# Two layers of mixer and expert stage on one core: modulation columns read two visits after their DMAs, and more ticks between the parts of the second mixer's coroutines

## The chip, the core and the metric

The kernel runs on one core of a Trainium2 chip. The metric is device time in microseconds for one launch, the median of several runs. The core has TensorE (PE for its matmuls, PEld for its weight loads), VectorE (DVE), ScalarE (ACT), GpSimd (POOL) and SyncE (SP), which here only issues DMAs. Each engine works through its own queue in order and waits on semaphores for the others.

## The reference, cut to what matters

Two layers over 512 tokens of width 1024, in fp32. The first layer's mixer is `mixer_ab` (a gated linear recurrence beside chunked gated linear attention), the second's is `mixer_c` (a gated delta rule with 8 heads of 128). Each layer ends in 32 experts in 4 groups, two experts per token.

```python
cond = silu(c)
for layer in range(2):
    mod = cond @ w_ada[layer] + b_ada[layer]          # 6 vectors of 1024 per layer
    sh1, sc1, gt1, sh2, sc2, gt2 = split(mod, 6)
    u = rms_norm(h, norm1[layer]) * (1 + sc1) + sh1
    m = mixer_ab(u, ...) if layer == 0 else mixer_c(u, ...)
    h = h + gt1 * m
    u = rms_norm(h, norm2[layer]) * (1 + sc2) + sh2
    h = h + gt2 * hier_moe(u, ...)                    # 32 experts, top 2 of one group
return rms_norm(h, final_norm)
```

In `mixer_c` each head solves a triangular system in every chunk, and then runs a recurrence over the chunks:

```python
v_new = u_c - w_c @ state
o     = (q * exp(g)) @ state + (q @ k.T * decay) @ v_new
state = state * exp(g_last) + (k * exp(g_last - g)).T @ v_new
o     = head_rms_norm(o, norm_g) * silu(z)            # then @ w_out
```

## The kernel before

**Steps and ticks.** A mixer is a list of steps, run in order by `run_steps` (line 491). A step splits a block of weights into a high and a low part (`split`, lines 423 and 424: ACT copies the high part, POOL subtracts to get the low one) and then issues matmuls of 128x512, three for each product (lines 430 to 432). After every six of these matmuls the step yields, which is one tick of the stream (`Stream`, line 49). All other work of a mixer is in Python generators, here called coroutines, which the stream resumes: a generator that yields n is resumed n ticks later. So a number behind a `yield` says how many groups of six matmuls are written into the program between one part of a coroutine and the next. Once the steps of a list are used up, `flush` and `until` go on ticking with no matmuls in between, until the generators that must be finished are finished.

**Order.** That fixes the order in which the program is written. A planner then puts each engine's instructions in order with its own costs, by the written order as priority among those that it holds to be ready, so small shifts against the written order occur. On the chip each engine's queue runs strictly in that order: an instruction whose input is late holds up everything behind it on its engine.

**Modulation vectors.** `mods` (line 317) works on the vectors (layer, index) that are not needed at once: six in the first mixer, four in the second. One vector takes four visits, in each of which eight small matmuls (line 258) multiply the condition into one 1 MB tile of `w_ada`. After the second and the fourth visit ACT copies 512 results into `modrow` (line 348) and issues two or four small DMAs (line 355) which gather them into rows of a stack tile `modst`, one buffer for each of two shapes. `finish` transposes the stack on PE (line 296 or 303) and lets DVE add it up into columns (lines 308 and 310). A vector is finished in the visit right after its fourth one (`made[0][0] < n`); visits are three or four ticks apart in the first mixer (`M0`), six in the second (`M1`). The last vector has no next visit: it is finished four ticks after its last one. Before the output projection `build` waits until the stream's queue is empty.

**Second mixer.** Its 20 units are k, q, z, v for four groups of two heads, and four quarters of the output projection; each unit of the first kind is 48 step matmuls per pair of tiles and heads, 8 ticks. The coroutines per head are `keys`, `queries` and `values`; `logits` computes the gates once and sets `gates_known`, for which `keys` waits. When a group's two heads have their keys, `solve` starts: it waits `g.wait` ticks (22, 22, 18, 22), then until the group before it has been solved, and then goes through five parts up to `recurrence`. For each of the four chunks after the first, `recurrence` has three parts: the state product (line 1186, with DVE's `rr_` at 1188), the solve (1195, with DVE's `vn` at 1197), and the outputs (1203, 1212, 1214); after the outputs it spawns `head_out`, which normalises on ACT and DVE (894 to 907), yields `HO`, transposes (911) and splits the result for the output projection (915 to 917). `head_out` serves the first mixer's attention as well. The last quarter of the output projection (`fin`, 48 step matmuls) is run by `build` after all coroutines of the mixer have ended, and brings in the router and the experts' pools.

**Experts.** `moe` runs 16 pairs of experts, lines 1455 to 1608; its weights come as 1 MB DMAs on SP's queue into 17 or so buffers as they come free.

Of the kernel before, what the change touches and what calls it, by code (L numbers as in the profile page):

```python
# [33 lines left out]
W0 = 8, 6  # L34
W1 = 10

LL, LK, K2, LV, LQ, HO, A1, A2, GL = 3, 5, 3, 6, 4, 3, 3, 2, 3
M0, M1 = (3, 4, 4), (6,)
WAIT = 22, 22, 18, 22

# [10 lines left out]
class Stream:  # L51
# [2 lines left out]


    def __init__(self):
        self.n, self.c, self.q, self.front = 0, 0, [], 0

    def spawn(self, gen, lag=0, back=False):
        self.front += not back  # L60
        self.push(gen, lag, back)
        self.run()

    def push(self, gen, lag, back):
        self.c += 1
        heapq.heappush(self.q, (self.n + lag, self.c, gen, back))

    def run(self):
        while self.q and self.q[0][0] <= self.n:
            _, _, gen, back = heapq.heappop(self.q)  # L70
            lag = next(gen, None)
            if lag is None:
                self.front -= not back
            else:
                self.push(gen, lag, back)

    def tick(self):
        self.n += 1
# [11 lines left out]
class Build:  # L90
# [224 lines left out]
    def mods(self, vs, pool, ahead, pace, then={}):  # L315


        seq = [(l, v, hb, i) for l, v in vs for hb in range(2) for i in range(2)]
        tiles = []

        def issue():
            if len(tiles) < len(seq):
                l, v, hb, i = seq[len(tiles)]
                src = self.a["w_ada"][l][512 * i:512 * i + 512, v * D + hb * 512:v * D + hb * 512 + 512]
                tiles.append(self.load(src, 512, pool))

        def finish():
            _, l, v, st = made.pop(0)
            self.mod_finish(l, v, st)
            if (l, v) in then:  # L330
                after.append(then[l, v])
        for _ in range(ahead):
            issue()
        made, after = [], []
        for n, (l, v, hb, i) in enumerate(seq):
            yield pace[n % len(pace)]
            if not i:
                p = self.ps()
            self.mod_rows(p, tiles[n], 4 * i, not i, i == 1)
            tiles[n] = None  # L340
            issue()
            while after:
                after.pop()()
            if made and made[0][0] < n:
                finish()
            if i:
                rows = self.mix.tile([P, 512], F32, name="modrow", tag="modrow")
                self.nc.scalar.activation(rows, p, AF.Copy)
                if not hb:
                    st = self.mod_stack(v)  # L350

                m, w = st.shape
                for j in range(m // 8):
                    r = m // 2 * hb + 4 * j
                    self.nc.scalar.dma_start(st[r:r + 4], rows[::32, w * j:w * j + w])
                if hb:
                    made.append((n, l, v, st))
        for _ in range(len(made)):
            yield 4
            finish()  # L360
        while after:
            yield 3
            after.pop()()

    def mod_stack(self, v):

# [553 lines left out]
    def mixer_c(self, u, es, right, second):  # L920
# [45 lines left out]
        def logits():  # L966

            p = self.narrow(u, wba)
            bap = ep.tile([P, T], F32, name="bap", tag="kn", bufs=1)
            nc.vector.tensor_copy(bap, p)  # L970
            yield 2
            p = self.ps([P, NT, 16])
            for t in range(NT):
                nc.tensor.matmul(p[:, t], bap[:, t * P:(t + 1) * P], self.fold[:, :16], start=True, stop=True)
            with tc.high_priority(PRI):
                nc.vector.tensor_add(xa_, p[:, :, 8:16], prm[:, None, 8:16].to_broadcast([P, NT, 8]))
                nc.vector.scalar_tensor_tensor(gd, xa_, -1.0, xa_, op0=OP.mult, op1=OP.max)
                nc.scalar.activation(gd, gd, AF.Exp, scale=-1.0)
                nc.scalar.activation(prm[:, 0:8], prm[:, 0:8], AF.Exp)
                nc.scalar.activation(beta, p[:, :, 0:8], AF.Exp, scale=-1.0)  # L980
                nc.scalar.activation(gd, gd, AF.Ln, bias=self.one)
            nc.vector.tensor_scalar(beta, beta, 1.0, None, op0=OP.add)
            nc.vector.reciprocal(beta, beta)
            nc.vector.scalar_tensor_tensor(gd, xa_, 0.0, gd, op0=OP.max, op1=OP.add)
            nc.vector.scalar_tensor_tensor(gd, gd, -1.0, prm[:, None, 0:8].to_broadcast([P, NT, 8]),
                                           op0=OP.mult, op1=OP.mult)
            yield LL
            with tc.high_priority(PRI):
                nc.vector.tensor_copy(gd40[:, :, 32:40], gd)
                p = self.ps([P, NT, 40])  # L990
                pl = self.ps([P, NT, 8])
                nc.tensor.matmul(p, tri, gd40, start=True, stop=True)
                nc.tensor.matmul(pl, self.ones, gd, start=True, stop=True)
                nc.vector.tensor_copy(gc40, p)
                pr = self.ps([40, T])
                for t in range(NT):
                    nc.tensor.matmul(pr[:, t * P:(t + 1) * P], gc40[:, t], self.ident, start=True, stop=True)
                nc.scalar.activation(grow, pr, AF.Copy)
                nc.vector.tensor_sub(grow[32:40], pr[32:40], grow[32:40].bitcast(F32))
            nc.vector.tensor_copy(egl, pl)  # L1000
            nc.vector.tensor_copy(egn, p[:, :, 0:8])
            nc.vector.tensor_sub(ehat, egl, gc)
            nc.scalar.activation(ex, ex, AF.Exp)
            nc.vector.tensor_scalar(egn, egn, -1.0, None, op0=OP.mult)
            self.gates_known = True
            first_columns()

# [62 lines left out]
        def queries(h, hd, p, g):  # L1070
            qT = conv_silu(p, h, "qT", ep)
            sq = ep.tile([P, T], F32, name="sq", tag="vT", bufs=1)
            nc.gpsimd.tensor_mul(sq, qT, qT)
            sums = self.column_sums(sq, ep)
            next(sums)
            yield LQ
            while not hd.keyed:
                yield 1
            nc.gpsimd.tensor_mul(hd.qg, hd.qg, qT)
            p = self.ps([P, NT, P])  # L1080
            for t in range(NT):
                nc.tensor.matmul(p[:, t], hd.kT[:, ts(t)], qT[:, ts(t)], start=True, stop=True)
            nc.vector.tensor_mul(hd.E, p, hd.E)
            p = next(sums)

            if g.eq is None:
                g.eq = hp.tile([P, NT, HG], F32, name="eq", bufs=3)
            nc.vector.tensor_scalar(g.eq[:, :, h % HG], p, P * EPS, P * EPS * EPS, op0=OP.mult, op1=OP.add)
# [11 lines left out]
        def solve(g):  # L1100
# [27 lines left out]
            for b in range(4):  # L1128
                src = Yt[sb[b]].rearrange("p c u -> p u c")
                nc.vector.transpose(XT[sb[b], :, sb[b]], src)  # L1130
                nc.scalar.activation(X[sb[b], :, sb[b]], src, AF.Copy)
            yield 1

            lo32 = slice(0, 32)
            pP = self.ps([P, U, 32])
# [37 lines left out]
        def recurrence(g):  # L1173
# [5 lines left out]
            for t in range(NT):  # L1179
# [8 lines left out]
                    nc.vector.scalar_tensor_tensor(r, p, hd.sc[:, 2, t:t + 1], hd.vb[:, t], op0=OP.mult, op1=OP.add)  # L1188
                    R.append(r)
                if t:  # L1190
                    yield 1
                VN = []
                for hh in range(HG):
                    p = self.ps([P, P])
# [616 lines left out]
    def build(self):  # L1811
# [4 lines left out]
        with ExitStack() as es0:  # L1816
# [8 lines left out]
            for l in range(2):  # L1825
                with ExitStack() as es:
                    self.mix = self.pool(es, "mix%d" % l, 2, **right_side)
                    self.whl = self.pool(es, "whl%d" % l, 3, **right_side)
                    right = self.pool(es, "right%d" % l, 1, **right_side)
                    self.stream = st = Stream()  # L1830
                    with ExitStack() as ms:
                        ut = [self.uroom.tile([P, 4, T], F32R, name="w", tag="w") for _ in range(4)]
                        u = lambda i, k, ut=ut: ut[2 * i + k // 4][:, k % 4]
                        vp = self.pool(ms, "v%d" % l, 2 - l)
                        us = ExitStack()
                        tmp = self.pool(us, "ut%d" % l, 1, **right_side)
                        if l == 0:
                            fin = self.mixer_ab(u, ms, right, *self.startup(u, tmp, us, vp))
                        else:
                            fin = self.mixer_c(u, ms, right, self.restart(u, tmp, us, vp))  # L1840
                        st.until(lambda: not st.q)
                    os_ = ExitStack()
                    self.moe_open(l, os_)
                    self.run_steps(st, fin)
                    st.until(lambda: not st.q)
                self.dump_h("hm%d" % l)
                self.moe(os_)
                if l:
                    self.finish()
                os_.close()  # L1850
                self.dump_h("ho%d" % l)
# [137 lines left out]
```

## Time and profile before

| what | value |
| --- | --- |
| median of 3 runs | 1714.82 us (1712.03 to 1715.41) |
| profiled execution | 1716.33 us, of which 1714.6 us are the span of the instructions |
| mean granted clock of TensorE | 0.978 of full speed |
| first mixer | from 0 to about 300 us |
| first expert stage | from about 320 to 800 us |
| second mixer | from about 815 to 1200 us |
| second expert stage | from about 1210 to 1700 us |
| DMA in the expert stages | 411 to 413 GB/s |

A row of the waits names the instruction that waited, what it waited for, and the time in total, how often, and the longest. A row of the timeline has the start, the duration, engine, line, operation, output<-input and shape; in brackets is the idle time of the engine before it. A matmul's duration includes its way through the array: matmuls start every 0.23 us while each is shown with 0.39 us.

### The profile page before, as it was taken

Reading aid. Unit: us, or ns where it says so; the run is one execution under the profiler, and the core shown is the slowest. Engines: PE = TensorE matmul, PEld = TensorE weight load, DVE = VectorE, ACT = ScalarE, POOL = GpSimd, SP = SyncE. Lnnn points to the kernel's source line nnn. Section 1 sums busy time; section 2 is a strip of 40 time slices with the busy share of each in tenths; the row PEclk is TensorE's granted clock in tenths of the full one; section 3 lists DMA queues with packets and bytes.
Section 4 is the critical chain, followed back from the end, with each engine's and each line's share of the span. In section 5 each row is a group of like instructions: output and inputs, shape, how many; then the busy total and the mean of one; then the engine's idle time right before and its main releaser. Section 6 shows DMA issues by size and latency. Waiting matters only on the chain. (4 is left out here: it accounts for less than half of the span.)

```text
span 1714.6 us, 23030 instructions
## 1 busy us (share of the span) xinstructions
PE 1630.9 (95%) x8890; PEld 979.8 (57%) x8890; DVE 766.4 (45%) x1770; ACT 522.6 (30%) x1033; POOL 396.1 (23%) x346
## 2 busy tenths in 40 slices
PE   6999998899999999998999999999899999999996
PEld 3665666544554555454666766778454555455453
DVE  3345543432433224244687787755424334243324
ACT  4665322310110111013746566554210111011013
POOL 2464442210010101001544343443110101001011
PEclk9999998999999999999899999999999999999998
DMA  8765645699999999995244433156689999999992
GB/s 304 228 222 170 248 149 196 233 361 379 412 413 411 414 411 413 413 411 172 75 138 134 149 99 122 52 187 246 255 355 409 413 411 413 412 412 413 412 406 99
DMA packets 156561, 496.02 MB, mean 289 GB/s; under 512 B 16472, under 2 KB 43668, under 8 KB 141088
## 3 DMA queue, kind: packets, MB, share of 16 engines
q1 hardware_dynamic: 155488, 493.23, 74.9%
q8 instruction: 72, 1.18, 0.3%
q10 hardware_dynamic: 960, 1.28, 0.2%
q14 instruction: 41, 0.34, 0.1%
HBM read 492.21 MB, written 2.10 MB: 288 GB/s over the span
## 5 line engine op out<-in xcount | busy, mean ns | idle before, releaser
L1531 PE MATMUL ps<-w,XTm 128*64 128x512 f32 x2048 | 447.2, 593 | 0.0
L1531 PEld LDWEIGHTS ps<-w,XTm 128*64 128x64 f32 x2048 | 161.7, 137 | 267.6 <-issue 260.5
L424 POOL TENSOR_TENSOR wlo<-w,whi 128x512 fp32r<-128x512 f32 x136 | 181.5, 1340 | 249.2 <-ACT whi L423 231.3
L1585 PE MATMUL ps<-w,hT 128*64 128x512 f32 (+1 forms) x1056 | 229.2, 583 | 1.0 <-ACT hT L1563 1.0
L1554 DVE TENSOR_TENSOR gg<-gg,ps 128x512 f32<-128x512 f32 x32 | 22.0, 689 | 377.4 <-PE ps L1531 377.3
L430 PE MATMUL ps<-w,whi 128*128 128x512 f32 x384 | 162.9, 425 | 0.7 <-ACT w L552 0.7
L431 PE MATMUL ps<-w,whi 128*128 128x512 f32 x384 | 154.6, 403 | 2.2 <-POOL w L554 1.5
L1585 PEld LDWEIGHTS ps<-w,hT 128*64 128x64 f32 x1056 | 81.8, 136 | 128.9 <-issue 116.0
L432 PE MATMUL ps<-w,wlo 128*128 128x512 f32 x384 | 154.1, 402 | 0.0
L1608 DVE TENSOR_TENSOR w<-w,ps 128x512 f32<-128x512 f32 (+1 forms) x248 | 149.4, 664 | 6.9 <-PE ps L1599 5.5
L1540 POOL CAST sel<-ident 32x128 fp32r<-32x128 f32 x32 | 9.0, 282 | 591.9 <-PE ps L1568 533.8
L1589 POOL TENSOR_TENSOR yl<-y,yh 128x512 fp32r<-128x512 f32 x60 | 76.6, 1276 | 249.6 <-ACT yh L1588 249.6
L1588 ACT ACTIVATE yh<-y 128x512 fp32r<-128x512 f32 (+1 forms) x66 | 40.8, 618 | 293.7 <-DVE y L1587 292.7
L423 ACT ACTIVATE whi<-w 128x512 fp32r<-128x512 f32 x136 | 84.6, 627 | 146.1 <-PE ps L431 76.0
L1455 PE MATMUL ps<-Dm,hhi 128*128 128x256 f32 x512 | 126.7, 289 | 0.0
L1455 PE MATMUL ps<-Dm,hlo 128*128 128x256 f32 x512 | 123.9, 284 | 0.0
L1587 DVE SCALAR_TENSOR_TENSOR y<-ps,wsl,gate 128x512 f32<-128x512 f32 (+1 forms) x66 | 48.5, 735 | 149.8 <-issue 76.2
L1455 PEld LDWEIGHTS ps<-Dm,hhi 128*128 128x128 f32 x512 | 101.9, 200 | 13.5 <-issue 13.5
L1599 PE MATMUL ps<-yh,dt 128*128 128x512 f32 (+1 forms) x264 | 105.9, 406 | 0.0
L1563 ACT ACTIVATE hT<-ps 128x512 f32<-128x512 f32 x32 | 19.1, 598 | 284.2 <-PE ps L1561 265.9
L1455 PEld LDWEIGHTS ps<-Dm,hlo 128*128 128x128 f32 x512 | 101.8, 199 | 0.2
L1599 PE MATMUL ps<-yl,dt 128*128 128x512 f32 (+1 forms) x264 | 100.9, 387 | 0.0
(522 smaller groups left out, 2356.4 us busy)
## 6 DMA issues: line engine op xcount, KB each, us to landing
w<-in_moe_w_dram SPq DMA_DIRECT2D x380, 1024.0 KB
w<-in_w_ada_dram SPq DMA_DIRECT2D x40, 1024.0 KB
w<-in_w_in_c_dram SPq DMA_DIRECT2D x16, 1024.0 KB
w<-in_w_in_ab_dram SPq DMA_DIRECT2D x10, 1024.0 KB
wst<-in_w_ada_dram SPq DMA_DIRECT2D x8, 1024.0 KB
w<-in_w_out_ab_dram SPq DMA_DIRECT2D x4, 1024.0 KB
w<-in_moe_w_dram SPq DMA_DIRECT2D x8, 512.0 KB
w<-in_w_out_c_dram SPq DMA_DIRECT2D x4, 1024.0 KB
```

Of the source, the lines that this page charges most:

```text
L423: nc.scalar.activation(hi, src, AF.Copy)
L424: nc.gpsimd.tensor_sub(lo, src, hi.bitcast(F32))
L430: mm(p, lhs[0], rhs[0], start=start, stop=False)
L431: mm(p, lhs[0], rhs[1], start=False, stop=False)
L432: mm(p, lhs[1], rhs[0], start=False, stop=stop)
L1455: nc.tensor.matmul(p, spread(src[:, t], k // 4)[k % 4], Dm[:, t].rearrange("p e s -> p (e s)"), start=t + i == 0, stop=t == NT - 1 and i == 1)
L1531: self.nc.tensor.matmul(ps[j][half[e]], X[:, k, half[e]], w, start=k == 0, stop=k == KD - 1)
L1585: nc.tensor.matmul(py[half[e]], hT[:, k, half[e]], w, start=k == 0, stop=k == 3)
L1587: nc.vector.scalar_tensor_tensor(y32, py, wsl, gate[:, c], op0=OP.mult, op1=OP.mult)
L1589: (nc.vector if last else nc.gpsimd).tensor_sub(yl[:, c], y32, yh[:, c].bitcast(F32))
L1599: mm = nc.tensor.matmul(p, dt[:, t * P:(t + 1) * P], y[:, s], start=i == 0, stop=i == 1)
L1608: nc.vector.tensor_add(h, h, p)
```

## The change

`mods` finishes a vector one visit later (`n - 1`), and hands the last vector to a generator `rest`, pushed with a lag of 8 ticks and marked `late`: `build` no longer waits for it before the output projection. The constant `HO` goes from 3 to 4. `logits` yields two ticks before it sets `gates_known`; `queries` yields two ticks between its product with the keys and the matmuls of its column sums; `solve` yields two ticks instead of one behind the copies into `X` and `XT`; `recurrence` yields two ticks instead of one between the state product and the solve, in the second to the fourth chunk. No instruction is added or removed.

```diff
-LL, LK, K2, LV, LQ, HO, A1, A2, GL = 3, 5, 3, 6, 4, 3, 3, 2, 3
+LL, LK, K2, LV, LQ, HO, A1, A2, GL = 3, 5, 3, 6, 4, 4, 3, 2, 3
...
-        self.n, self.c, self.q, self.front = 0, 0, [], 0
+        self.n, self.c, self.q, self.front, self.late = 0, 0, [], 0, 0
...
-    def push(self, gen, lag, back):
+    def push(self, gen, lag, back, late=False):
         self.c += 1
-        heapq.heappush(self.q, (self.n + lag, self.c, gen, back))
+        self.late += late
+        heapq.heappush(self.q, (self.n + lag, self.c, gen, back, late))
...
-            if made and made[0][0] < n:
+            if made and made[0][0] < n - 1:
                 finish()
...
-        for _ in range(len(made)):
-            yield 4
-            finish()
-        while after:
-            yield 3
-            after.pop()()
+
+        def rest():
+            while made or after:
+                while after:
+                    after.pop()()
+                if made:
+                    finish()
+                yield 6
+        self.stream.push(rest(), 8, True, True)
...
             nc.vector.tensor_scalar(egn, egn, -1.0, None, op0=OP.mult)
+            yield 2
             self.gates_known = True
...
             nc.vector.tensor_mul(hd.E, p, hd.E)
+            yield 2
             p = next(sums)
...
                 nc.scalar.activation(X[sb[b], :, sb[b]], src, AF.Copy)
-            yield 1
+            yield 2
...
                 if t:
-                    yield 1
+                    yield 2
                 VN = []
...
-                        st.until(lambda: not st.q)
+                        st.until(lambda: len(st.q) == st.late)
                     os_ = ExitStack()
```

## Rows read from the trace of the kernel before

**Rows 1.** The page's busy times by engine, with their share of the span.

```profile
PE 1630.9 (95%) x8890; PEld 979.8 (57%) x8890; DVE 766.4 (45%) x1770; ACT 522.6 (30%) x1033; POOL 396.1 (23%) x346
```

**Rows 2.** The page's costliest groups: the experts' matmuls; last figure: idle before.

```profile
L1531 PE MATMUL ps<-w,XTm 128*64 128x512 f32 x2048 | 447.2, 593 | 0.0
```

**Rows 3.** Waits of PE in the first mixer, 45 to 300 us.

```profile
PE ps L303 <- DMA modst<-modrow: 4.8, 1, 4.8
PE ps L296 <- DMA w<-in_w_ada_dram: 2.9, 1, 2.9
```

**Rows 4.** Waits of PE in the second mixer, 760 to 1200 us.

```profile
PE ps L284 <- DVE xr L280: 3.9, 6, 1.2
PE ps L911 <- ACT orow L907: 2.4, 2, 1.9
PE ps L1139 <- ACT X L1131: 2.3, 2, 2.0
PE ps L1038 <- DVE grow L999: 2.0, 1, 2.0
PE ps L1195 <- DVE rr__7207 L1188: 1.6, 1, 1.6
...
PE ps L303 <- DMA modst<-modrow: 0.8, 1, 0.8
...
PE ps L1195 <- DVE rr__8078 L1188: 0.5, 1, 0.5
```

**Rows 5.** Stretches: length, busy time by engine, granted clock (sixth), DMA share, GB/s.

```profile
148.60:151.50 2.90, 0.02 (x1) 0.00 (x0) 2.90 (x5) 1.11 (x4) 2.02 (x1) 0.99 0.73 283
151.50:154.90 3.40, 3.36 (x9) 2.78 (x10) 3.40 (x8) 2.96 (x6) 1.92 (x2) 0.50 0.01 2
...
264.10:274.30 10.20, 5.40 (x15) 4.04 (x15) 1.94 (x9) 0.63 (x1) 1.26 (x1) 0.50 1.00 413
...
847.80:854.60 6.80, 6.80 (x18) 4.88 (x17) 4.90 (x15) 6.73 (x16) 4.56 (x5) 0.50 0.33 116
...
1021.90:1028.70 6.80, 6.04 (x19) 4.87 (x19) 5.15 (x23) 0.78 (x3) 0.01 (x1) 0.50 0.03 8
...
1127.70:1131.10 3.40, 3.40 (x12) 2.71 (x11) 0.83 (x3) 1.76 (x8) 1.56 (x2) 0.50 0.00 0
```

**Rows 6.** Timeline of all engines at the end of the first mixer.

```profile
258.34 0.16 DVE L409 SCALAR_TENSOR_TENSOR or<-rsz,or 128x4 f32<-128x4 f32 x1
...
258.86 1.30 POOL L424 TENSOR_TENSOR wlo<-w,whi 128x512 fp32r<-128x512 f32 x1 [2.30 <-ACT whi L423]
...
258.93 1.24 DVE L409 SCALAR_TENSOR_TENSOR or<-rsz,or 128x4 f32<-128x4 f32 x1
...
262.52 2.37 ACTq L355 DMA_DIRECT2D modst<-modrow  x4
...
263.82 1.25 PE L911 MATMUL ps<-ident,orow 128*128 128x128 f32 x4 [2.00 <-DVE orow L905]
...
267.06 1.26 POOL L917 TENSOR_TENSOR yBlo<-yf,yBhi 128x512 fp32r<-128x512 f32 x1 [4.17 <-ACT yBhi L916]
```

**Rows 7.** PE by line, 1175.55 to 1194.6 us; one of three like rows.

```profile
L430 PE MATMUL ps<-whi,ychi 128*128 128x512 f32 x18 | 7.3, 405 | 0.0
```

**Rows 8.** Timelines at the end of the second mixer: PE, ACT, POOL.

```profile
1170.80 0.39 PE L1214 MATMUL ps<-Sc,qg 128*128 128x128 f32 x2
...
1175.16 0.38 PE L911 MATMUL ps<-ident,orow 128*128 128x128 f32 x2
...
1172.65 0.62 ACT L907 ACTIVATE orow<-ps,or 128x128 f32<-128x128 f32 x2 [0.23 <-DVE or L901]
...
1177.10 0.73 POOL L917 TENSOR_TENSOR yclo<-yf,ychi 128x256 fp32r<-128x256 f32 x1 [1.05 <-ACT ychi L916]
```

**Rows 9.** Timelines of DVE and ACT around the fourth z tile of the second mixer.

```profile
959.98 0.34 DVE L915 SCALAR_TENSOR_TENSOR yf<-ps,cv,Z 128x128 f32<-128x128 f32 x1
...
960.79 0.60 ACT L1233 ACTIVATE Z<-ps 128x512 f32<-128x512 f32 x1
```

More of the change, by code (lines that the diff above doesn't have):

```diff
@@ L62, in spawn @@
         self.run()
-    def push(self, gen, lag, back):
+    def push(self, gen, lag, back, late=False):
         self.c += 1
-        heapq.heappush(self.q, (self.n + lag, self.c, gen, back))
+        self.late += late
+        heapq.heappush(self.q, (self.n + lag, self.c, gen, back, late))
     def run(self):
         while self.q and self.q[0][0] <= self.n:
-            _, _, gen, back = heapq.heappop(self.q)
+            _, _, gen, back, late = heapq.heappop(self.q)
+            self.late -= late
             lag = next(gen, None)
@@ L74, in run @@
             else:
-                self.push(gen, lag, back)
+                self.push(gen, lag, back, late)
     def tick(self):
```

## The prediction

> **What bounds the kernel now.** I read the page's busy times first: PE is busy in 1630.9 of 1714.6 us, twice as long as the next engine, DVE [rows 1]. PE's matmuls in the experts have no idle time before them [rows 2], so that stage lasts as long as its matmuls, and whatever a mixer saves reaches the end of the kernel. The 84 us in which PE is idle are the place to look; the waits of PE, asked for each mixer alone, say what ends them. In the first mixer two waits stand out, both ahead of transposes of a modulation stack, 4.8 and 2.9 us [rows 3]. The second is put down to a load of `w_ada`, but the instruction reads only `modst` and a constant, so I read it as a wait for the small DMAs into `modst`. In the second mixer the waits are spread over the places that the change touches: column sums 3.9 us, the `head_out` transposes 2.4, the solve's first products 2.3, the gates' rows 2.0, the chunks' solves four times from 1.6 to 0.5, together 3.7, and one modulation stack 0.8 [rows 4]. That is 15.1 us.
>
> A wait costs more than itself. The stretches show the granted clock falling to 0.50, the lower of its two levels (1.2 GHz), for a while behind such a gap: right behind the 2.9 us one, behind the one of 4.8, and at four places of the second mixer [rows 5]. Work done at half clock takes twice its time, so half of PE's busy time in such a stretch is lost: 1.7 us of 3.36 in the first; in the second mixer half of 6.80, 6.04 and twice 3.40 (the row of one of these two stands), together 9.8 us.
>
> **The change part by part.** No instruction is added. Each yield puts six more step matmuls, 6 x 0.23 = 1.4 us at full clock, between an instruction and the one that reads it.
>
> *A vector finished one visit later, first mixer.* The transposes at 151.5 us [rows 3, 5] move behind the next visit, three or four ticks and so 4 us or more later, when their data has landed. Gone: 2.9 us of wait and 1.7 us of clock, 4.6. Below: 0, if the late data was that of another queue and the next instruction waits for it; above: 4.6. I take 4.6, since the DMAs are what the transpose reads. The stack has one buffer per shape, so for three of the ten vectors the next vector's small DMAs now wait for the transpose of the same visit, and behind them ACT's next `split` copy; the transpose follows that visit's matmuls while ACT still copies `modrow`, so nothing (bounds 0 and 3 x 0.3). The router's preparation, which runs behind the vector of shifts, comes one visit later, at 14 of 24, still far ahead of the router. On SP's queue nothing changes its order, since the loads are asked for in the visit before `finish` in either version.
>
> *The first mixer's last vector.* Its four DMAs leave ACT from 262.52 to 264.89 us; PE ends its `head_out` transposes at 265.07 [rows 6] and then stands for 4.8 us in front of the stack [rows 3], with the output projection's last quarter queued behind. With `rest` the transpose comes 8 ticks later, inside that quarter, and costs there the 0.28 us that it costs now. The projection can start at 265.07 instead of 270.1. What is late next is `yBlo` of the last chunk, ready at 268.32 [rows 6]; but nine matmuls for the other three chunks come first, which take some 3.4 us at half clock (nine in the 3.40 us from 151.5 on [rows 5]), and only the third matmul behind them reads it. So 5.0 us are gained. Of the half-clock stretch [rows 5] the matmuls from 270.09 on lie in it for 4.2 us, so 2.1 are lost now; the gap of 2.0 us ahead of the transposes [rows 6] stays, and elsewhere a gap of this size is followed by at least 3.4 us at half clock [rows 4, 5]: from 264.1 on, that leaves 2.4 us of the new start in it, 1.2 lost. Net 5.0 + 2.1 - 1.2 = 5.9. Below: 2.0, if the quarter is held up by something else for 3.9 us; above: 7.1, if no half clock remains. I take 5.7, the sum less the 0.2 us for a late `yBlo`.
>
> The Trainium skill (DMA: Bandwidth & Descriptors, Anatomy of one DMA) puts the fixed part of a DMA at about 2.0 us, most of it the receipt of the last write. By that figure, an estimate, the stack would have been there at 266.9, the wait would be 1.8 us and the gain 3 us smaller; the trace shows 5.0 us from the last issue to the transpose, and it decides.
>
> *`HO` 4 in the first mixer.* It moves transposes whose results are read only in the last quarter: nothing; a tick of 1.4 us either way bounds it.
>
> *Second mixer.* I go wait by wait [rows 4] and let a yield cover 1.4 us of each. Column sums, two ticks, all six at most 1.2: 3.9 gone. Chunk solves, one tick: 3.5 of 3.7. `X`, one tick: 1.7 of 2.3. `head_out`, one tick: 1.9 of 2.4. Gates, two ticks: 2.0. Last vectors: 0.8. Together 13.8. Of the 9.8 us of clock I count half, 4.9, since a gap that only gets shorter may still be followed by half clock. That is 18.7 if each wait was only a matter of distance. It is not: PE waits where DVE, ACT and the splits are crowded, and there an instruction may be late by another full tick. What that costs no row shows directly; bounds are 0 and 24.9 (all waits and all of the clock). The nearest row is DVE's three-operand instruction on 128x4 numbers, which takes 0.16 us alone and 1.24 beside a POOL subtraction of 1.30 that started with it [rows 6]. That is about one tick, as much as most yields add. So I take half: 9.4 us.
>
> *What the longer chain costs.* The four groups wait for each other. Three chunks with one more tick, the solve's tick and `head_out`'s add up: by the code, group 2's recurrence starts on its values, as now, and ends three ticks later; group 3, which now starts just when group 2 ends (later than its own wait of 18 to 22 ticks), starts three later, and its own chain is one (`solve`), three (chunks) and one (`HO`) longer. That would be eight ticks for the last transposes; the order in which the two generators are polled takes one back: seven. Now they stand at 1175.16 us [rows 8], and from then on there are 3 x 18 = 54 step matmuls [rows 7], of which 48 are the last quarter: one tick of cover. So six ticks fall behind the last step, where ticks hold no matmuls. PE then goes, with nothing else written in between, through the last chunk's solve, `vn`, outputs, `head_out` and transposes. From the end of the outputs at 1171.19 to `orow` at 1173.27 are 2.1 us, from the end of the transposes at 1175.54 to `yclo` at 1177.83 2.3 us [rows 8]. Of the latter, nine matmuls of the other chunks (2.0 us) cover all but 0.3. Idle is 2.1 + 0.3 and some 0.35 for `vn`, 2.75 us; a gap of that size brings half clock, 1.7 us or more [rows 5]: 4.5. Below: 0, if the planner puts matmuls of the last quarter into the holes, for which two chunks are ready. I take 3, nearer the upper end, because the first mixer's end has the same kind of hole and the planner left it open [rows 6].
>
> *Sum.* 4.6 + 5.7 + 9.4 - 3 = 16.7 us off the profiled execution's 1716.3 (1714.6 of span and 1.7 around it): 1699.6. That execution lies 1.5 us above the median of the runs, so I forecast 1698.
>
> **The rivals.** *The waits come back.* In the second mixer a longer distance helps only where the producer is late by a fixed time. If it is late because DVE and POOL get in each other's way [rows 6], or if the planner, finding nothing else ready, moves the instruction forward again, the waits reappear behind the same lines. For it: 1.24 us instead of 0.16 for the same instruction. Against: the column sums' six waits are short and follow one producer. Then only the first mixer's 10.3 remain, less the 3 of the chain: 1716.3 - 7.3 - 1.5 = 1707.5. The Trainium skill (SBUF — State Buffer, its single rule) has the cause of it: VectorE and GpSimd share a port pair under an exclusive lock, and the loser waits for the whole instruction; the 1.24 us row agrees.
>
> *All of it goes*: both mixers' waits and clock, 10.3 + 24.9, and the planner fills the end: 1716.3 - 35.2 - 1.5 = 1680.
>
> *The chain becomes the bound, and the kernel slower.* Place: group 0 to the end of the second mixer. The fourth `z` tile takes a buffer that `head_out` of group 0 frees only with its last `yf`; now ACT writes it at 960.79, right behind that read [rows 9], and until then the projection's result keeps one of eight PSUM banks. By the code that hold grows from three ticks to about ten. PE stood still in that crowd of ticks already, 1.6 us at `rr` and 1.2 at the sums as the longest of each [rows 4]; a bank fewer for seven ticks may cost 5 more. With the end's holes all open, 4.7 us with the weight splits late too, and 5 us of clock behind them, that is 15 us, against 10.3 from the first mixer and none from the second: 1719. It decides from 10.3 us on. Against: the planner interleaves wherever something is ready.
>
> *The change doesn't do what it says*: the planner puts the transposes back to where the data is late, and the rest evens out: 1715.
>
> **How the numbers follow.** The forecast 0.50, the waits back 0.20, all gone 0.10, no effect 0.09, slower 0.11. The forecast's own terms reach from 4.6 + 2.0 + 4 - 4.5 = 6 to 4.6 + 7.1 + 16 = 28 us, 1687 to 1709. The range of 1684 to 1712 adds the second rival whole, and of the others the parts near it. About 0.2% (3.4 us) is what a measurement of this kernel can tell from no change. Faster: 0.50 + 0.20 + 0.10 = 0.80; same 0.09; slower 0.11.
>
> **What would show it.** In the waits of PE after: no row of a `modst` transpose over 1 us in either mixer, the first mixer's projection starting within 1 us of the `head_out` transposes, a shorter half-clock stretch there; the column sums gone from the list, the chunk solves' rows below 0.6; in the second mixer's end, a wait for `orow` ahead of the last quarter of some 2 us. The prediction is wrong if the time between the second mixer's first step and the last quarter is not at least 5 us shorter, or if a row of PSUM or of `Z` stands for more than 4 us there.

## The result, and the profile after

The changed kernel takes 1698.36 us, the median of five runs (1694.91 to 1700.37), beside 1714.82 for the kernel before (1712.03 to 1717.14): ratio 0.9895, 95% interval 0.9883 to 0.9907. The forecast was 1698. The total is right; the experiments show that a good part of the reasoning behind it is not.

The page's head and its busy line, of the kernel after:

```profile
span 1698.2 us, 23027 instructions
...
PE 1623.4 (96%) x8890; PEld 973.7 (57%) x8890; DVE 766.6 (45%) x1770; ACT 522.6 (31%) x1034; POOL 398.7 (23%) x346
```

Set against [rows 1] this parts the gain in two. The 8890 matmuls are the same, so the 7.5 us by which PE is busy for less are clock; idle time, span less busy, falls from 83.7 to 74.8 us, by 8.9.

PE's waits after, first in the first mixer (45 to 300 us), then in the second (760 to 1187 us):

```profile
PE ps L437 <- POOL wlo L429: 2.1, 2, 1.7
PE ps L916 <- DVE orow L910: 2.0, 1, 2.0
PE ps L260 <- DMA w<-in_w_ada_dram: 1.5, 2, 1.0
...
PE ps L436 <- POOL wlo L429: 1.0, 2, 0.7
```

```profile
...
PE ps L916 <- ACT orow L912: 3.1, 3, 1.9
PE ps L1035 <- ACT kT L1020: 2.6, 1, 2.6
PE ps L1088 <- ACT qT L1020: 2.0, 2, 1.4
PE ps L1210 <- DVE vn L1204: 1.9, 2, 1.4
PE ps L1146 <- ACT X L1138: 1.4, 1, 1.4
PE ps L1202 <- DVE rr__7220 L1195: 1.4, 1, 1.4
PE ps L1193 <- DVE Sc L1215: 1.1, 1, 1.1
...
```

Both waits ahead of the stacks [rows 3] are gone, and so are column sums and gates [rows 4]. New are `kT` and `vn`; the waits for `qT` (1.0 us before) and, in the first mixer, for `wlo` (0.4) have grown. Line numbers are those of each run's own kernel: the solve's first products stand at L1139 before, at L1144 in E1 and at L1146 after. Without the start of the mixer (`hn`, 7.2 us in both), the second mixer's waits add up to 15.5 us, before to 19.6.

To see where time is won I set the n-th step matmul of the one kernel against the n-th of the other; the difference of their starts is the lead. Over the former stall at 148.6 us the lead rises from -0.8 to 5.8 us; at 196 us it is only 0.7, at 252 us 2.8, 9.0 in the output projection, 8.6 at the first mixer's end. The experts run at the same pace in both (+0.5). In the second mixer the lead grows from 9.1 to 25.0 us until four ticks ahead of the last quarter, and is 16.1 at the end. So the first mixer gave 8.6 us, the second 7.0.

Stretches of the kernel after (length; busy time of PE, PEld, DVE, ACT, POOL; granted clock; DMA):

```profile
148.00:152.00 4.00, 3.57 (x15) 2.56 (x15) 4.00 (x5) 2.25 (x4) 3.44 (x2) 1.00 0.81 263
...
838.00:848.20 10.20, 9.92 (x23) 6.71 (x24) 7.62 (x18) 9.18 (x20) 4.34 (x5) 0.50 0.26 90
...
1158.80:1162.20 3.40, 3.40 (x9) 2.66 (x10) 0.62 (x3) 0.58 (x2) 0.72 (x1) 0.50 0.99 405
```

The half clock of [rows 5] behind 148 us is gone, as are the three stretches between 1021 and 1131 us. At 838 us it is 3.4 us longer than before, and 1158.8 is new, behind the chain that now ends late. PE there:

```profile
1154.84 0.49 PE L1202 MATMUL ps<-rr__9746,XT 128*128 128x128 f32 x2 [0.60 <-DVE rr__9746 L1195]
...
1158.77 0.45 PE L916 MATMUL ps<-ident,orow 128*128 128x128 f32 x1 [1.90 <-ACT orow L912]
```

### The profile page after: what moved, and what is told of

Read it like the earlier page. It is cut to its first block, busy times and chain, and to the rows that moved or that the text cites. A ratio compares the mean times of both kernels' runs of the same rounds, so it can differ in the third digit from the quotient of the medians.

```text
span 1698.2 us, 23027 instructions
## 1 busy us (share of the span) xinstructions
PE 1623.4 (96%) x8890; PEld 973.7 (57%) x8890; DVE 766.6 (45%) x1770; ACT 522.6 (31%) x1034; POOL 398.7 (23%) x346
## 5 line engine op out<-in xcount | busy, mean ns | idle before, releaser
L429 POOL TENSOR_TENSOR wlo<-w,whi 128x512 fp32r<-128x512 f32 x136 | 185.9, 1374 | 233.7 <-ACT whi L428 230.9
```

The source lines that it names most:

```text
L429: nc.gpsimd.tensor_sub(lo, src, hi.bitcast(F32))
```

## The experiments

Each was timed beside the kernel before, whose median was then 1714.8 to 1716.5; the ratio is to that one. "Vectors" is the change of `mods` with `rest`; "ticks" are the five edits from `HO` to the chunks. The profile columns are one execution each: PE busy and idle, the wait for `X` in the solve of the third group (group 2), and the length of the half-clock stretch that begins in the 10 us behind it.

| kernel | median us | ratio to before (95%) | PE busy | idle | wait for X | half clock |
| --- | --- | --- | --- | --- | --- | --- |
| before | 1714.8 | | 1630.9 | 83.7 | 2.3 | 3.4 |
| after | 1698.4 | 0.9883 to 0.9907 | 1623.4 | 74.8 | 1.4 | none |
| E1 vectors | 1714.7 | 0.9981 to 1.0003 | 1629.5 | 83.0 | 2.8 | 13.7 |
| E2 ticks | 1713.8 | 0.9980 to 1.0004 | 1634.9 | 86.7 | 2.9 | 10.2 |
| E3 later visit | 1719.5 | 1.0014 to 1.0035 | 1635.1 | 85.7 | 2.8 | 17.1 |
| E4 last vector | 1711.3 | 0.9953 to 0.9977 | 1628.8 | 81.6 | 2.3 | 3.4 |
| E5 all but solve's tick | 1706.4 | 0.9927 to 0.9955 | 1630.8 | 79.6 | 3.3 | 13.7 |
| E6 vectors + solve's tick | 1700.0 | 0.9896 to 0.9922 | 1620.0 | 77.8 | 1.5 | none |
| E7 all but `HO` 4 | 1712.0 | 0.9963 to 0.9982 | 1632.6 | 83.8 | 2.8 | 10.2 |
| E8 all but later visit | 1709.1 | 0.9930 to 0.9966 | 1630.3 | 78.3 | 2.9 | 3.4 |
| E9 solve's tick | 1711.5 | 0.9962 to 0.9982 | 1628.1 | 83.3 | 1.4 | 3.4 |
| E10 vectors, X by POOL | 1704.1 | 0.9923 to 0.9963 | 1623.2 | 78.0 | none | 3.4 |
| E11 after, X by POOL | 1696.0 | 0.9869 to 0.9912 | 1621.5 | 76.2 | none | none |
| E12 E11, short end | 1696.1 | 0.9867 to 0.9900 | 1619.8 | 72.3 | none | none |

The profiled executions of E2, E5 and E7 lie 10, 6 and 6 us above their medians; their columns say where, not how much.

**The parts alone (E1 to E4).** E1 has the edits of `mods`, `rest`, `late`; E2 the others; E3 and E4 split E1:

```diff
-            if made and made[0][0] < n:       # E3: this line alone; E4: all of E1 but this line
+            if made and made[0][0] < n - 1:
```

E1: 

> The modulation part alone: a vector finished one visit later and the last one inside the output projection; all tick counts as before. Theory: the change is a sum of parts that lie in different stretches. The two traces put 8.6 us on the first mixer, so this kernel should be 8.6 to 9.4 us faster than before (the second mixer adds at most the 0.8 us wait of its last vector), and its second mixer should last as long as before within 1.5 us. Rival: the first mixer's gain needs the longer HO as well; then less than 6 us.

E2: 

> The tick counts alone (HO 4, the two ticks in logits, queries, solve and recurrence); the modulation vectors finished as before. Theory: 7.0 us faster, all of it in the second mixer (the two traces' difference there), the first mixer within 1 us of before. Rival (the waits come back): the ticks give nothing of their own, within 3 us of before, and the second mixer's gain in the two traces hung on the vectors being finished later.

E3: 

> Only the condition n - 1: each vector finished one visit later, but the last one still four ticks after its last visit, ahead of the output projection. Theory: the 4.6 us of the stall at 148.6 us are gained and partly given back within the next 40 us, since PE then runs into the weight splits and the loads of w_ada: 2 to 4 us faster. Rival: all 4.6 stay, or more.

E4: 

> Only the last vector's move into the output projection; the others finished in the next visit as before. Theory: 5.5 to 6.5 us faster, all of it between the head_out transposes and the output projection's first matmuls of the first mixer, and the stall at 148.6 us still there. Rival: another wait takes the stack's place there, and less than 3 us remain.

Neither part reached its forecast, and the parts do not add up: E1 is 1.2 us and E2 2.2 us under the kernel before that was timed beside them (1715.96), neither a shown gain, and 16.5 us together. E2 came out within the 3 us of its rival, with a first mixer that is 3.3 us longer in its trace. In E1 the first mixer gains 8.0 us, as forecast, and the experts keep it; in the second the lead is still 10.9 us until the solve of group 2 and 4.3 behind it. E1's wait there, and the stretch that follows:

```profile
PE ps L1144 <- ACT X L1136: 2.8, 2, 2.1
```

```profile
1050.30:1064.00 13.70, 13.15 (x135) 9.89 (x136) 4.92 (x18) 7.97 (x18) 3.17 (x3) 0.50 0.47 154
```

Half of PE's 13.15 busy us is 6.6 us of loss. E3, slower than before, has the same place, with the longest stretch of all:

```profile
1059.30:1076.40 17.10, 16.41 (x145) 11.98 (x145) 7.34 (x24) 8.78 (x20) 4.37 (x5) 0.50 0.38 124
```

E3 is a miss in the first mixer too: its lead behind the stall is gone again by the mixer's end (-0.1 us). E4 met its expectation in place but not in size: the drain ahead of the projection is worth 6.2 us in its trace, the kernel is 4.7 us faster, and between ticks 110 and 140 of the second mixer the lead falls from 7.7 to 4.2 us.

That gave theory A: the second mixer's gain hangs on the wait for `X`.

**Theory A: with and without the solve's tick (E5, E6, E9).** The same edit, taken from the changed kernel, added to the vectors, and made alone:

```diff
                 nc.scalar.activation(X[sb[b], :, sb[b]], src, AF.Copy)
-            yield 1
+            yield 2          # E5: back at 1; E6: 2, on E1; E9: 2, on the kernel before
```

E5: 

> The changed kernel without the solve's tick (that yield gives 1 again). Theory A (what the change is worth in the second mixer hangs on the one wait for the solve's X: 1.4 us and full clock behind it in the changed kernel, 2.0 us and 3.4 us of half clock before, 2.1 to 2.9 us and 10 to 17 us of half clock where only a part was made): the wait is back at 2 us or more with over 10 us of half clock behind it, so 0.7 + 5 or more: about 1704 us, 1702 to 1708. Theory B (each tick covers its own wait and no more): 1.4 us slower, 1699.8. Theory C (the stretch behind X is set by how the whole tail happens to be ordered): any time, and X's wait does not tell the length of the half clock.

E6: 

> The vectors' part (a vector finished a visit later, the last one's during the output projection) and of the six ticks only the solve's. The vectors alone took 1714.7. Theory A: X's wait falls under 1.6 us and the 13.7 us of half clock behind it go: 6 to 8 us faster, 1707 to 1709. Theory B: one tick, 1.4 us: 1713.3. Theory C: X's wait may shrink and the half clock stay, so no forecast closer than 1700 to 1715.

E9: 

> The kernel before with the solve's first yield at 2 and nothing else changed. With the vectors' part that tick was worth 14.7 us. Theory A (it takes out the wait for X, and what that wait costs depends on the half clock behind it): in the kernel before the wait is 2.3 us with 3.4 us of half clock behind it, so 1.4 + 1.7 = 3 us faster, 1713. Rival (the tick itself moves the rest of the mixer into a better order, with or without the vectors): 10 to 15 us faster, 1701 to 1706.

One tick is worth 8.0 us in the changed kernel, 14.8 on the vectors alone, 3.3 to 4.8 on the kernel before (by the median in the table, or by the one timed beside it, 1716.3). E5 went with theory A: `X` is late again, and between ticks 96 and 104 of the mixer, where group 2's `X` is read, E5 falls 8.1 us behind the changed kernel. E6 and E9 went with it only in part. E6 gained twice what theory A allows: its lead over E1 grows by 7.5 us at ticks 96 to 104, but by 6.4 already at ticks 80 to 88. E9's sum agrees with theory A by luck: in its trace ticks 96 to 104 give 1.1 us and ticks 80 to 88 give 7.1, part of which is lost again later. That is what the rival said, which named 10 to 15. In the kernel before, PE stands at ticks 80 to 88 for column sums, the state product and `rr_`, and the half clock of 1021.9 us follows [rows 5]:

```profile
1019.20:1022.90 3.70, 1.60 (x13) 0.95 (x12) 3.70 (x13) 2.12 (x3) 2.71 (x3) 0.86 0.72 247
```

E9 has no half clock there, and these two waits are what is left of column sums and of `X` (900 to 1200 us):

```profile
PE ps L1139 <- ACT X L1131: 1.4, 1, 1.4
...
PE ps L284 <- DVE xr L280: 0.4, 1, 0.4
```

The changed kernel, too, gains 7.5 us of lead at ticks 80 to 88 and 0.7 at ticks 96 to 104. So `X` is where versions with a part of the change lose time; it is not where the changed kernel gets ahead. What the solve's tick does at ticks 80 to 88 no run tells, and a lead over some ticks also holds work that has only moved into or out of them. E6's wait and the 20 us behind it:

```profile
PE ps L1144 <- ACT X L1136: 1.5, 2, 1.4
```

```profile
1044.00:1064.00 20.00, 19.85 (x211) 14.17 (x210) 12.95 (x37) 16.15 (x32) 7.81 (x8) 1.00 0.33 106
```

From E1 to E6 the page's PE busy time falls by 9.5 us and the idle time by 5.2: two thirds of what this tick gave was clock. With the vectors and this one edit of the five the kernel takes 1700.0 us, with all of them 1698.4.

**Why X is late.** ACT before, from the gates' exponential to the copies of `X`:

```profile
1053.37 1.28 ACT L1053 ACT_TABLE_LOAD   x1
1054.67 0.63 ACT L1053 ACTIVATE E<-E 128x512 f32<-128x512 f32 x1
1055.32 1.28 ACT L1014 ACT_TABLE_LOAD   x1
1056.61 0.63 ACT L1014 ACTIVATE kT<-kT 128x512 f32<-128x512 f32 x1
1057.25 1.28 ACT L1056 ACT_TABLE_LOAD   x1
1058.54 0.60 ACT L1056 ACTIVATE qg<-ps 128x512 f32<-128x512 f32 x1
1059.04 0.62 ACT L423 ACTIVATE whi<-w 128x512 fp32r<-128x512 f32 x1
1059.56 2.02 ACT L1131 ACTIVATE X<-Yt 32x256 f32<-32x256 f32 x3
```

Nothing here waits, and three function tables are loaded for 3.84 us. The input `Yt` was there 9 us earlier: DVE's transposes of the same data, written beside the copies, began at 1050.41 us. After the change `kT` comes ahead of `E`, whose table serves `qg` too, and a load falls away:

```profile
1037.13 1.28 ACT L1020 ACT_TABLE_LOAD   x1
1038.43 0.63 ACT L1020 ACTIVATE kT<-kT 128x512 f32<-128x512 f32 x1
1039.08 1.28 ACT L1059 ACT_TABLE_LOAD   x1
1040.37 0.63 ACT L1059 ACTIVATE E<-E 128x512 f32<-128x512 f32 x1
1040.91 0.58 ACT L1062 ACTIVATE qg<-ps 128x512 f32<-128x512 f32 x1
...
1042.21 2.69 ACT L1138 ACTIVATE X<-Yt 32x256 f32<-32x256 f32 x4
```

E6 keeps all three loads and waits no longer (1.5 us), so the load that falls away is not what the tick gives. By these rows the wait is a matter of ACT's queue and not of the chain. E10 and E11 try that by taking the copies off ACT:

```diff
-                nc.scalar.activation(X[sb[b], :, sb[b]], src, AF.Copy)
+                nc.gpsimd.tensor_copy(X[sb[b], :, sb[b]], src)   # E10: on E1; E11: on the changed kernel
```

E10: 

> The vectors' part alone (1714.7 us), no tick added, but the four copies that write X are done by POOL's tensor_copy, not by ACT, where they stood behind three loads of a function table (1.28 us each), an exponential, two products and the split's copy. Theory A (X is late because ACT's queue is, and its wait brings the long half clock): the wait of 2.8 us goes and with it most of the 13.7 us at half clock, 7 to 10 us faster: 1705 to 1708, or down to 1700 as with the solve's tick. Rival (X is late for the whole chain, or the half clock comes from the order of the tail): within 3 us of 1714.7.

E11: 

> The changed kernel with the four copies that write X on POOL. Theory A: its last wait for X, 1.4 us, goes, and nothing else, since no half clock follows it there: 1697, 1694 to 1699. Rival (POOL's copies hold up DVE's transposes beside them and the splits behind them): 2 us or more slower than the changed kernel.

E10, without any added tick, is 10.6 us faster than E1. In it DVE, POOL and PE:

```profile
1035.89 2.73 DVE L1135 STREAM_TRANSPOSE XT<-Yt 32x256 f32<-32x256 f32 x4
1035.92 2.84 POOL L1136 COPY X<-Yt 32x256 f32<-32x256 f32 x4 [1.51 <-DVE Yt L1129]
...
1040.67 0.69 PE L1144 MATMUL ps<-X,LT 32*32 32x32 f32 x32
```

`X` is there 1.9 us before PE reads it. From tick 96 to 104 of the mixer E1 falls back by 6.6 us and E10 moves ahead by 1.0: 7.6 of the 10.6. The rest is not `X`: in the first mixer, which is the same in both, E10's profiled execution has 3.4 us of half clock and E1's 10.2. E11's median is 2.4 us under the changed kernel's; the intervals overlap, so a gain is not shown, but the rival's loss isn't there.

**The other parts taken out (E7, E8).**

```diff
-LL, LK, K2, LV, LQ, HO, A1, A2, GL = 3, 5, 3, 6, 4, 4, 3, 2, 3      # E7
+LL, LK, K2, LV, LQ, HO, A1, A2, GL = 3, 5, 3, 6, 4, 3, 3, 2, 3
...
-            if made and made[0][0] < n - 1:                            # E8
+            if made and made[0][0] < n:
```

E7: 

> The changed kernel with HO back at 3. The ticks alone lost 3.1 us in the first mixer at a wait for orow of 2.07 us with 6.8 us of half clock behind it, which the kernel before does not have. If HO is what made that wait (theory A), the first mixer is 2 to 3 us shorter and the second one to two longer by its wait for orow (2.4 before): 1696 to 1699. If HO covers the second mixer's wait for orow as I forecast (theory B, 1.9 us) and is worth nothing in the first: 1700.2.

E8: 

> The changed kernel with the vectors in a visit finished one visit behind, as before (n instead of n - 1); the last vector's part and the six ticks stay. The 2.9 us wait at 148 us comes back in the first mixer. Theory A (the later visit gave its 4.4 us back within the same mixer and alone made the second mixer's order worse by 6 us at X): 1694 to 1700, no slower than the changed kernel. Theory B (the stall's gain is real and adds up): 4.6 us slower, 1703. The parts run alone would give 1714.8 - 4.5 - 2.0 = 1708 if they added.

E7 refutes both theories: `HO` back at 3 costs 13.7 us. Its waits, 900 to 1200 us:

```profile
PE ps L916 <- ACT orow L912: 12.2, 8, 3.1
PE ps L1146 <- ACT X L1138: 2.8, 1, 2.8
```

`head_out` waits eight times there, 12.2 us instead of 3.1, and `X` is late again though the solve has its tick. With `HO` 3 and the other distances of the kernel before it was 2.4 us [rows 4], in E6 4.5: three ticks are too few for `orow` once the other ticks are in; which of them does it no run tells. E7's profiled execution is 18.0 us behind the changed kernel's, 4.4 of them in the first mixer and 5.9 at ticks 96 to 104, but one execution is not sure to better than 2 to 4 us there (E11, with the first mixer of the changed kernel, lies 1.8 behind it).

E8 refutes theory A for the later visit: 10.7 us slower, though the same line alone (E3) makes the kernel 3.5 slower. In the trace 5.5 us are the first mixer, with the wait of [rows 3] back; its row now names the small DMAs, as I had read it:

```profile
PE ps L298 <- DMA modst<-modrow: 3.2, 1, 3.2
```

```profile
152.20:159.00 6.80, 6.41 (x16) 5.10 (x17) 6.80 (x15) 4.72 (x9) 3.21 (x2) 0.50 0.00 1
```

**A shorter end (E12).** On E11, for the last group only:

```diff
-            yield 2                       # solve, and the chunks of recurrence
+            yield 2 if g.i < NG - 1 else 1
```

> The changed kernel with X written by POOL, and in the last of the four groups the solve's and the chunks' yields back at 1, so that its chain is four ticks shorter. Theory A (the longer chain costs what stands at the end: waits of 0.6 and 1.9 us and 1.7 us of half clock, 4.2 in all, and most of it goes with four ticks): 2 to 4 us faster than with X by POOL alone, 1692 to 1694. Rival (the shorter distance brings back as much in the last group, its waits for rr of 0.5 to 1.4 us at four chunks): 1696 or more.

In the trace the end does shorten: the lead given back from four ticks ahead of the last quarter on is 4.1 us, with E11 7.3; no half clock stands there, and the last wait is

```profile
1152.37 0.33 PE L916 MATMUL ps<-ident,orow 128*128 128x128 f32 x1 [0.82 <-ACT orow L912]
```

Some of that is lost just ahead, so that from tick 140 on E12 gains 1.8 us on E11. The medians, 1696.1 and 1696.0 (four and six runs, spread over 4 and 13 us), don't show it; 1696 or more is what the rival said. Both lie some 2 us under the changed kernel, which is no shown difference either.

## Why the prediction was right, point by point

*First mixer: 10.3 us forecast, 8.6 found.* The last vector: 5.7 against 6.2, with projection matmuls starting within 0.1 us of the first `head_out` transpose, and 3.4 us at half clock where there were 10.2. The stall: the wait and its clock went, 6.6 us of lead with what is moved behind, where I had 4.6; but 5.1 of it came back in the next 35 us. I asked what the transposes would do later, and not what PE would meet at once if it came sooner: the split's low part from POOL, the wait of 1.7 us for `wlo` above, and then tiles of `w_ada`. Ahead of the drain 2.8 us are left.

*Second mixer: 9.4 less 3 forecast, 7.0 found.* The chain's cost was named rightly: 0.6 and 1.9 us of idle and 1.7 of clock, 4.2 against 3. By subtraction the gross gain is 11.2, inside my bounds. Its makeup is another. Column sums and gates went as forecast, and the solve's first products nearly so (1.4 left, 0.6 forecast), but one of the chunks' solves still waits 1.4, `kT` and `vn` wait where nothing did, `qT` waits longer, and the `head_out` transposes, which were to lose 1.9 of 2.4, still wait 1.2 beside the 1.9 of the chain. At ticks 80 to 88, the largest step, my terms come to some 3.6 us (column sums 1.0, `rr_` 1.1, half of the clock's 3.0); the lead grew by 7.5. At `X` I forecast 1.7 and half of 1.7 of clock, and 0.7 came. Of the net 7.0 us idle time gave 4.1 (19.6 to 15.5), clock the other 2.9: the stretches of 1021.9 and 1127.7 [rows 5] and the like one at 1062.8 have no successor (half of 6.04, 3.40 and 3.40 is 6.4 us), and at 838 and 1158.8 us 1.6 and 1.7 were lost.

*The step that failed* is "I go wait by wait [rows 4] and let a yield cover 1.4 us of each". It treats the edits as a sum. I gave the solve's tick 1.7 us and measured 14.8, 8.0 or 3 to 5, as the rest stood; `HO`'s tick 1.9 us, and 13.7; the later visit 4.6, and 10.7 or -3.5. A part alone would have been forecast badly; the total came out because what the terms left out went both ways, and that it came within half a microsecond is luck. I had read `X`'s row as a chain too short by a tick, and it is a queue: the rows of ACT above would have told it, had I asked what ACT did in the 9 us since `Yt`.

*The signs.* No `modst` row, the projection's start, sums gone, a wait for `orow` of 1.9 us at the end: as forecast. Chunk solves below 0.6: wrong, 1.4. The mixer before the last quarter is 15.8 us shorter (5 was the mark; part of that is only moved behind).

*The rivals.* "The waits come back" is true in part, 15.5 of 19.6 us stand, at other lines; but it counted no clock. "All of it goes" missed. The slower one had its chain, at less than half of its price (2.5 us of idle and 1.7 of clock; I had 4.7 and 5), but not its decisive term: no row of `Z` or of PSUM stands in the waits. The Trainium skill (SBUF — State Buffer, its single rule), from which I took one cause, holds the lock of the port pair to DVE instructions with two SBUF inputs or in a two-port mode; E10 agrees for the case left out: DVE's four transposes of `XT` take 2.73 us beside POOL's copies and 2.69 in E1 without them.

*Open.* What sets the length of a half-clock stretch: waits for `X` of 2.3 to 3.3 us were followed by 3.4, 10.2, 13.7 and 17.1 us, and waits of 2.9 by 3.4 in E8 and 10.2 in E2. Nor is it known what the solve's tick does at ticks 80 to 88. Nor was it tried why the later visit, alone a loss, is worth 10.7 us with the rest.

## What to carry to other kernels

Ask of a late operand what its engine did since the input was there: if a queue stands ahead of it (here three table loads), move the copy to an idle engine before buying distance with ticks. A wait's price is the wait and the clock behind it, so compare PE's busy time between versions with the same matmuls; here it was nearly half of the gain. A forecast that comes true in total can still be wrong in place (E9): compare the n-th step of both versions, and see where the time is won. Edits to a written order are no sum: take each out of the whole as well as making it alone, since here the same line was worth 14.8 us in one place and 3 to 5 in another.

## What was not expected of the hardware

In one place the clock fell without a gap before it. In E10, PE is by its records busy for all of 3.5 us, and then the granted clock is at half (1.2 GHz) for 3.4:

```profile
1046.00:1049.50 3.50, 3.50 (x85) 2.92 (x84) 2.52 (x6) 1.19 (x8) 3.50 (x4) 0.99 0.56 170
1049.50:1052.90 3.40, 3.40 (x33) 2.66 (x21) 2.92 (x16) 3.01 (x8) 1.25 (x3) 0.50 1.06 371
```

What PE did ahead of the fall were small matmuls, the last of them 64 products of 32x32 in the solve. And one order had two clocks: the first mixer of E1 and E10, the same in both, had 10.2 and 3.4 us at half clock, and E10 came out of it 3.8 us sooner.
